# Experts of a two-layer decoder on one core: from split float32r products to plain float32 products on column tiles

## The chip, the cores and the metric

One core of a Trainium2 chip runs the whole program. The metric is the time of one execution on the device in microseconds (us); each number of a run is one execution, and a profile is one execution more, recorded instruction by instruction. Engines: TensorE (PE, with its weight loads as PEld), VectorE (DVE), ScalarE (ACT), GpSimd (POOL) and SyncE (SP), whose queue issues the loads.

## The reference

Two layers of a decoder over 256 tokens of 1024 channels. Each layer has four attention mixers and then a feed-forward part; in layer 0 that is a SwiGLU, in layer 1 it is eight SwiGLU experts of hidden width 2816, of which each token uses the two with the highest router logits. The change is in the experts alone:

```python
def moe_swiglu(h, router_w, w1, w3, w2):
    xt = h.reshape(-1, d)
    logits = (xt @ router_w).astype(jnp.float32)
    top_v, top_i = lax.top_k(logits, TOP_K)            # 2 of 8
    gate = jax.nn.softmax(top_v, axis=-1)
    ...
    a = lax.ragged_dot(xs, w1, sizes)
    g = lax.ragged_dot(xs, w3, sizes)
    y = lax.ragged_dot(jax.nn.silu(a) * g, w2, sizes)
    y = y * gate.reshape(-1)[order][:, None]
    return jnp.zeros_like(xt).at[tok].add(y)
```

Everything is float32. With the inputs of the reference the experts get 56, 55, 64, 69, 62, 65, 64 and 77 tokens.

## The kernel before, in words

Layer 1's experts are the function `moe`. It finds each token's two experts, gives every token a slot in each of them (`pos`), and **gathers** the tokens of two experts at a time by products with one-hot matrices (`onehot`, `gather`): `X(e)` is 1024 channels (8 blocks of 128) by 128 slots. An expert's 2816 hidden columns are worked in 11 steps of 256 (`j`); 88 pairs (expert, step) follow each other in the list `pairs`.

One step goes **up**, turns, and goes **down**. `up_half` multiplies the 128 slots (stationary operand) with the step's columns of `w1` and `w3` side by side (moving, 512 columns) over the 8 channel blocks into one PSUM bank `uv`. ScalarE and VectorE make silu(a) * g of it (`es`). `flip_act` turns the 128 x 256 result by two transposes (`at`), and `down` multiplies it with the step's 256 rows of `w2`, into two banks `y` that add up over the 11 steps. Behind the last step `scale_y` weights the rows with the gates, and `scatter_steps` adds them to the tokens (`scm`, then `xT`). The order is written out by hand: while step i goes up, step i-1 is turned between the halves of the up products and goes down after them; the flips, the scatter of the expert before and the gather of the next two hang on the lists `side` and `more`, one piece per step.

**Precision.** PE's fast type float32r keeps fewer bits than float32. So every operand is split into a high and a low float32r part, and every product is made of three (`mm3`, line 645: high by high, high by low, low by high). A weight tile comes from HBM as `raw` (128 x 2048 floats, 1 MiB); the class `Stream` loads the tiles in the order of a list `plan` into slots as these come free, and splits them in halves ahead of need (`ensure`): ScalarE writes `wh`, VectorE `wl = raw - wh`. The slot is free when its second half is split.

```python
    self.clk.sc.activation(wh[:, :hn], src, AF.Copy)
    self.clk.dv.tensor_tensor(wl[:, :hn], src, wh[:, :hn].bitcast(F32), op=OP.subtract)
```

**More than 128 tokens.** At the very end `mxv`, the largest count, is read into a register (line 1878), and a branch on all engines (line 1879) works slots 128 to 255 of every expert if it is above 128. With these inputs it is jumped over.

A recording layer (`Clock`, `Timed`) notes every operation, so nearly all instructions have line 385 in the profile; they are told apart by their tiles' names.

Of the kernel before, what the change touches and what calls it, by code (L numbers as in the profile page):

```python
# [26 lines left out]
P = 128  # L28
# [9 lines left out]
SLOTS = 128  # L38
NEG = -1e30
# [98 lines left out]
class Stream:  # L138
# [4 lines left out]
    def __init__(self, clk, plan):  # L143
# [7 lines left out]
        for ci, (key, ap) in enumerate(plan):  # L151
            assert key not in self.index, key
            self.index[key] = ci
            self.pieces += [(key, 0), (key, 1)]
# [16 lines left out]
    def add_halves(self, pool, names, last=None):  # L171

        for n in names:
            self.limit["wh" + n] = len(self.plan) if last is None else self.index[last]
            self.wring.appendleft((pool, n))
            self.look += 1
# [50 lines left out]
    def ensure(self, upto):  # L227

        while self.nsplit < min(upto, len(self.pieces)):
# [5 lines left out]
            while self.limit["wh" + self.wring[0][1]] < self.index[key]:  # L235
# [4 lines left out]
            wh = pool.tile([P, CH // 2], F32R, name=f"wh{self.nsplit}", tag="wh" + tag)  # L240
            wl = pool.tile([P, CH // 2], F32R, name=f"wl{self.nsplit}", tag="wl" + tag)
# [256 lines left out]
def trunk(ctx, tc, A):  # L498
# [41 lines left out]
    def add_item(it):  # L540
# [11 lines left out]
        elif k == "w2":  # L552
            add(it, ko(A["ffn_w2"][0, it[2] * 256:(it[2] + 1) * 256]))
        elif k == "e13":
            add(it, A["moe_w13"][0, l, it[2], it[3]])
        elif k == "e2":
            add(it, ko(A["moe_w2"][0, l, it[2] * 256:(it[2] + 1) * 256]))
# [29 lines left out]
    NSLOT, NWH, NWX, NX = 3, 4, (0, 0), (4, 5)  # L587
# [217 lines left out]
    hh = cpool.tile([P, KD, S], F32R, name="hh")  # L805
    hl = cpool.tile([P, KD, S], F32R, name="hl")
# [819 lines left out]
    def moe(fp, nf, gap, consts):  # L1626
# [8 lines left out]
        xe = mb.tile([P, 2, KD, SLOTS], F32R, name="xe", tag="merged")  # L1635
        half = lambda e: 0 if e % 2 == 0 else 1 + e // 2 % 2

        def X(e):

            if half(e) == 2:  # L1640
                return xe[:, 0], xe[:, 1]
            c = slice(half(e) * SLOTS, (half(e) + 1) * SLOTS)
            return hh[:, :, c], hl[:, :, c]
# [32 lines left out]
        st.move("aux")  # L1676
        for d in range(4, KD):
            flip(d)
# [24 lines left out]
        st.presplit(("e13", 0, 0, 1), 2)  # L1703
# [3 lines left out]
        cnti = fp.tile([P, 1], I32, name="cnti")  # L1707

        def gates():
# [3 lines left out]
            dv.tensor_copy(cnti, cnt[:, 0:1])  # L1713
            dv.tensor_tensor(w[:, :, 1:2], t8[:, :, 1:2], t8[:, :, 0:1], op=OP.subtract)
# [13 lines left out]
        def flip_oh(e, tag, res):  # L1728

            def f():  # L1730
                ps = pt(f"rt{tag}{e}")
                for i in range(2):
                    pe.matmul(ps[:, i * P:(i + 1) * P], ohv[:, i, e % 2], idr, start=True, stop=True)
                for i in range(2):
                    pe.matmul(ps[:, S:S + 1], ohv[:, i, e % 2].bitcast(F32), gat[:, i, e:e + 1], start=(i == 0),
                              stop=(i == 1))
                ohT = ohs[:, 512 + e % 2 * S:512 + (e % 2 + 1) * S]
# [5 lines left out]

        def gather(e):

            def pick(b, n):
                def f():
                    first = e == 0
                    ps = (px if first and n else pt)(f"g{e}{b}{n}")
                    for t in range(2):  # L1750
                        d = 2 * b + t
                        for i in range(2):
                            pe.matmul(ps[:, t * S:(t + 1) * S], (th, tl)[n][:, i, d * P:(d + 1) * P],
                                      ohv[:, i].rearrange("p e s -> p (e s)"), start=(i == 0), stop=(i == 1))
                    v = ps.rearrange("p (t e s) -> p t e s", t=2, e=2)
                    for k in range(2):
                        o = X(e + k)[n][:, 2 * b:2 * b + 2, :]
                        if first and n:
                            dv.tensor_copy(o, v[:, :, k])
                        else:  # L1760
                            sc.activation(o, v[:, :, k], AF.Copy)
                return f

            return [pick(b, n) for b in range(4) for n in range(2)]
# [12 lines left out]
        def scatter_steps(yy, ohT, tag, final=None):  # L1777
            def part(b):
                def f():
                    ps = pt(f"sc{tag}{b}")  # L1780
                    yh, yl = yy[b // 2]
                    for t in range(2):
                        o = ((2 * b + t) % 4) * P
                        pe.matmul(ps[:, t * S:(t + 1) * S], yh[:, o:o + P], ohT, start=True, stop=False)
                        pe.matmul(ps[:, t * S:(t + 1) * S], yl[:, o:o + P], ohT, start=False, stop=True)
# [15 lines left out]
        state = {0: {}, 1: {}}  # L1801
# [4 lines left out]
        side = deque([lambda: (gap.fill(4 - gap.j), st.move("gap")), flip_oh(0, "m", state[0]), lambda: deque(gap.end(), 0), flip_oh(1, "m", state[1])])  # L1806
        more = deque()
        ybanks, acts, atT = {}, {}, {}

        def up_half(e, j, c, ps):  # L1810

            Xh, Xl = X(e)
            for h, (wh, wl) in enumerate(st.halves(("e13", e, j, c))):
                whv = wh.rearrange("p (k n) -> p k n", k=2)
                wlv = wl.rearrange("p (k n) -> p k n", k=2)
                for k in range(2):
                    kk = 4 * c + 2 * h + k
                    mm3(ps, Xh[:, kk, :], Xl[:, kk, :], whv[:, k, :], wlv[:, k, :],
                        start=(kk == 0), stop=(kk == KD - 1))

        def flip_act(e, j):
            a = acts.pop((e, j))
            p2 = pt(f"at{e}_{j}")
            for t in range(2):
                pe.transpose(p2[:, t * P:(t + 1) * P], a[:, t * P:(t + 1) * P], ident)
            at = sm.tile([P, 512], F32R, name=f"ath{e}_{j}", tag="sq", bufs=3)
            ath, atl = at[:, 0:256], at[:, 256:512]
            sc.activation(ath, p2[:, 0:256], AF.Copy)
            dv.tensor_tensor(atl, p2[:, 0:256], ath.bitcast(F32), op=OP.subtract)
            atT[(e, j)] = (ath, atl)  # L1830

        def down(e, j):
            if j == 0:
                ybanks[e] = [px(f"y{e}_{n}") for n in range(2)]
            ath, atl = atT.pop((e, j))
            for h, (wh, wl) in enumerate(st.halves(("e2", e, j))):
                for n in range(2):
                    mm3(ybanks[e][n], ath[:, h * P:(h + 1) * P], atl[:, h * P:(h + 1) * P],
                        wh[:, n * 512:(n + 1) * 512], wl[:, n * 512:(n + 1) * 512],
                        start=(j == 0 and h == 0), stop=(j == NF - 1 and h == 1))  # L1840

        for i, (e, j) in enumerate(pairs):
            if j == 0 and e % 2 and e + 1 < NE:
                more.append(lambda e=e: onehot(e + 1, 0))
                more.extend(gather(e + 1))
            ps = pm(f"uv{e}_{j}")
            up_half(e, j, 0, ps)
            if i:
                flip_act(*pairs[i - 1])
            up_half(e, j, 1, ps)  # L1850
            s = sm.tile([P, 512], F32, name=f"es{e}_{j}", tag="sq", bufs=3)[:, 0:256]
            sc.activation(s, ps[:, 0:256], AF.Silu)
            dv.tensor_tensor(s, s, ps[:, 256:512], op=OP.mult)
            acts[(e, j)] = s
            if side:
                side.popleft()()
            if i:
                e2, j2 = pairs[i - 1]
                down(e2, j2)
                if j2 == NF - 1:  # L1860
                    yy = scale_y(ybanks.pop(e2), state[e2]["gs"], f"m{e2}")
# [219 lines left out]
```

## Time and profile before

| | us |
|---|---|
| runs of the kernel (median of 3) | 1577.34, 1573.70, 1574.76 (1574.76) |
| the profiled execution's own time | 1573.86 |
| its span, first to last instruction | 1572.1 |
| PE busy | 1532.2 (97%) |
| DVE busy | 1272.2 (81%) |
| ACT busy | 1037.2 (66%) |
| mean granted TensorE clock | 0.993 of full speed |

Busy time is the time in which an engine had at least one instruction under way; overlapping matmuls are not counted twice, while a mean of one counts each from its start to its end. So "mean 392" beside a product every 235 ns means that they overlap. "128*64" in a row of PE is rows by columns of the stationary operand, "128x256" what is written. Idle time of an engine that bounds nothing costs nothing.

### The profile page before, as it was taken

The numbers are of one execution on the slowest core, as the hardware profiler recorded it, in microseconds if no ns is written. First come the engines' busy times: TensorE is split into PE (matmuls) and PEld (weight loads), VectorE is DVE, ScalarE is ACT, GpSimd is POOL, SyncE is SP. The second block draws the span as 40 slices with busy tenths as digits, with TensorE's granted clock in tenths as the row PEclk, the third lists the DMA queues.
The fourth block names the chain that finished last, engine by engine and source line by source line (L and its number), as shares of the span: only waits on it lengthen the run. The fifth ranks groups of instructions, "written<-read, shape, count | busy, mean of one in ns | idle before, by whom it ended". The sixth has DMA issues, their size and how long they took to land.

```text
span 1572.1 us, 25486 instructions
## 1 busy us (share of the span) xinstructions
PE 1532.2 (97%) x10164; PEld 1352.0 (86%) x10164; DVE 1272.2 (81%) x1646; ACT 1037.2 (66%) x1452; POOL 56.2 (4%) x58
## 2 busy tenths in 40 slices
PE   7999998999999999999999999999999999999996
PEld 6998998899998999989778888888888888888885
DVE  4797787666656786776689989999899998999996
ACT  3546553544444546554678888888888888888884
POOL 0000013000001000012000000000000000000000
PEclk9999999999999999999999999999999999999998
DMA  9565656977633765539789999999899999999960
GB/s 370 222 232 185 223 207 245 367 269 252 233 135 113 258 215 188 188 135 355 288 334 371 356 338 365 357 363 354 330 365 356 365 355 335 359 363 363 366 243 29
DMA packets 84878, 445.99 MB, mean 284 GB/s; under 512 B 8080, under 2 KB 8464, under 8 KB 51344
## 3 DMA queue, kind: packets, MB, share of 16 engines
q1 hardware_dynamic: 84032, 443.71, 76.0%
q8 instruction: 81, 1.33, 0.3%
q10 hardware_dynamic: 720, 0.59, 0.1%
q14 instruction: 45, 0.37, 0.1%
HBM read 443.22 MB, written 1.05 MB: 283 GB/s over the span
## 4 chain that ended last, share of the span: by engine, by line
PE 79%; issue 15%; DVE 3%; DMA 1%; ACT 1%; POOL 1%; SPq 0%; DVEq 0%; POOLq 0%; ACTq 0%
PE uv L385 31%; PE y L385 15%; PE mg L385 11%; PE pt L385 7%; PE br L385 2%; PE at L385 1%; PE wo L385 1%; PE g L385 1%; PE scm L385 1%; DVE wl L385 1%; PE pcq L385 1%; PE ada L385 1%; PE pck L385 1%; PE oa L385 1%; DMA aux<-in_nsa_ck_w 0%
## 5 line engine op out<-in xcount | busy, mean ns | idle before, releaser
L385 DVE TENSOR_TENSOR wl<-raw,wh 128x1024 fp32r<-128x1024 f32 x738 | 883.9, 1228 | 168.7 <-ACT wh L385 157.0
L385 ACT ACTIVATE wh<-raw 128x1024 fp32r<-128x1024 f32 x738 | 769.7, 1056 | 142.6 <-PE uv L385 18.5
L385 PE MATMUL y<-wh,ath 128*128 128x512 f32 x704 | 232.9, 392 | 0.5 <-ACT ath L385 0.5
L385 PE MATMUL uv<-wh,hh 128*128 128x512 f32 x528 | 212.9, 403 | 0.0
L385 PE MATMUL uv<-wh,hl 128*128 128x512 f32 x528 | 207.0, 392 | 0.0
L385 PE MATMUL uv<-wl,hh 128*128 128x512 f32 x528 | 206.7, 392 | 0.0
L385 PEld LDWEIGHTS y<-wh,ath 128*128 128x128 f32 x704 | 132.1, 188 | 28.1 <-ACT ath L385 0.7
L385 PE MATMUL mg<-hh,wh 128*128 128x256 f32 x512 | 147.0, 287 | 0.8 <-DVE brt L385 0.8
L385 PE MATMUL mg<-hh,wl 128*128 128x256 f32 x512 | 143.5, 280 | 4.2 <-DVE wl L385 4.2
L385 PE MATMUL mg<-hl,wh 128*128 128x256 f32 x512 | 143.0, 279 | 0.0
L385 PE MATMUL y<-wl,ath 128*128 128x512 f32 x352 | 137.6, 391 | 0.0
L385 PE MATMUL uv<-wh,xe 128*128 128x512 f32 x352 | 119.1, 401 | 0.0
L385 PEld LDWEIGHTS uv<-wh,hl 128*128 128x128 f32 x528 | 99.1, 188 | 22.5
L385 PEld LDWEIGHTS uv<-wh,hh 128*128 128x128 f32 x528 | 99.2, 188 | 18.5
L385 PEld LDWEIGHTS uv<-wl,hh 128*128 128x128 f32 x528 | 99.4, 188 | 18.0
L385 PEld LDWEIGHTS mg<-hh,wl 128*128 128x128 f32 x512 | 96.5, 188 | 4.9 <-DVE wl L385 4.8
L385 PEld LDWEIGHTS mg<-hh,wh 128*128 128x128 f32 x512 | 96.6, 189 | 3.0 <-issue 2.0
L385 PEld LDWEIGHTS mg<-hl,wh 128*128 128x128 f32 x512 | 96.7, 189 | 1.0 <-issue 1.0
L385 PE MATMUL pt<-wh,hh 128*128 128x256 f32 (+1 forms) x320 | 90.3, 282 | 0.0
L385 PE MATMUL pt<-wl,hh 128*128 128x256 f32 (+1 forms) x320 | 89.2, 279 | 0.0
L385 PE MATMUL pt<-wh,hl 128*128 128x256 f32 (+1 forms) x320 | 89.2, 279 | 0.0
L385 PEld LDWEIGHTS uv<-wh,xe 128*128 128x128 f32 x352 | 66.2, 188 | 14.5
(417 smaller groups left out, 2837.5 us busy)
## 6 DMA issues: line engine op xcount, KB each, us to landing
raw<-in_moe_w SPq DMA_DIRECT2D x263, 1024.0 KB, 5.1
raw<-in_w_in SPq DMA_DIRECT2D x54, 1024.0 KB, 5.1
aux<-in_w_ada SPq DMA_DIRECT2D x48, 1024.0 KB, 7.4
raw<-in_ffn_w SPq DMA_DIRECT2D x33, 1024.0 KB, 5.4
raw<-in_w_branch SPq DMA_DIRECT2D x8, 1024.0 KB, 5.4
raw<-in_w_out SPq DMA_DIRECT2D x8, 1024.0 KB, 5.0
raw<-in_w_in_tail SPq DMA_DIRECT2D x2, 576.0 KB, 4.0
xT<-in_x SPq DMA_DIRECT2D x1, 1024.0 KB, 6.2
```

The costliest lines, as they stand in the source:

```text
L385: r = f(*args, **kw)
```

## The change

It does six things, all in layer 1's experts but for the tile of the split halves.

1. **Plain float32 products.** The expert weights (`e13`, `e2`) are no longer split; PE reads the raw tiles. `X(e)` is one float32 tile, gathered in one piece. A slot is freed (`raw_done`) when the products that read it are done.
2. **Two column tiles.** 64 slots (`BASE`) are the stationary operand of the base products. A step's 256 columns are two groups of 128 (`w1` and `w3` together 256 moving columns); group 0 stands on columns 0 to 63 of the array and writes partitions 0 to 63, group 1 on columns 64 to 127. Going down, the same with the two halves of the step's hidden columns.
3. **Arms.** Slots 64 to 95 and 96 to 127 are worked in two nested arms of 32 slots, on four column tiles, per block of two steps. Their products stand behind a comparison with the expert's own count (`regs[e]`, loaded into a register of PE alone); the other engines don't branch, they turn and evacuate the arms' banks (`uvo`, `yo`), which are cleared first, either way. An expert has 11 such places: 6 blocks, one last down part, four parts of the scatter.
4. **Slots.** The four tiles of split halves (now one tile `w` each) and `merged` become slots of the raw tiles in this stage; the tiles of the feed-forward pool are 4 instead of 5.
5. **Layout.** `moe_w13` and `moe_w2` are laid out anew on the host side so that a tile is 128 rows of 8 KB and the two groups are contiguous.
6. The early splits (`presplit`) of the first expert tiles are left out.

```diff
+BASE, MORE = 64, 32
+RAW = ("e13", "e2")
...
+            if key[0] not in RAW:
+                self.pieces += [(key, 0), (key, 1)]
...
-    NSLOT, NWH, NWX, NX = 3, 4, (0, 0), (4, 5)
+    NSLOT, NWH, NWX, NX = 3, 4, (0, 0), (4, 4)
...
+        st.add_slots(wpool, [f"w{i}" for i in range(NWH)])
+        st.add_slots(mb, ["merged"])
...
+        def flip_more(e, res):
...
+                for r in range(2):
+                    oh = columns(e, f"o{r}{e}", BASE + r * MORE, MORE)
+                    ps = pt(f"ro{r}{e}")
+                    for i in range(2):
+                        pe.matmul(ps[:, i * P:(i + 1) * P], oh[:, i], idr, start=True, stop=True)
...
+                    base(0)
+                    if rest is not None:
+                        reg, yo, oho = rest
+                        q = slice(MORE * b, MORE * (b + 1))
+
+                        def add(r):
+                            for t in range(2):
+                                pe.matmul(ps[:, t * S:(t + 1) * S], yo[q, r * S + t * P:r * S + (t + 1) * P],
+                                          oho[q, r, :], start=False, stop=False, tile_position=(MORE * b, 0))
+
+                        arms(reg, add)
+                    base(1)
...
+        def arms(reg, work, back=False):
+
+            with tc.If(reg > BASE):
+                if not back:
+                    work(0)
+                with tc.If(reg > BASE + MORE):
+                    work(1)
+                if back:
+                    work(0)
...
         def up_half(e, j, c, ps):
 
-            Xh, Xl = X(e)
-            for h, (wh, wl) in enumerate(st.halves(("e13", e, j, c))):
-                whv = wh.rearrange("p (k n) -> p k n", k=2)
-                wlv = wl.rearrange("p (k n) -> p k n", k=2)
-                for k in range(2):
-                    kk = 4 * c + 2 * h + k
-                    mm3(ps, Xh[:, kk, :], Xl[:, kk, :], whv[:, k, :], wlv[:, k, :],
-                        start=(kk == 0), stop=(kk == KD - 1))
+            x = X(e)
+            for kk in range(4 * c, 4 * c + 4):
+                w = raw13(e, j, kk)
+                for t in range(2):
+                    pe.matmul(ps[t * BASE:(t + 1) * BASE, 0:S], x[:, kk, 0:BASE], w[:, t], start=(kk == 0),
+                              stop=(kk == KD - 1), tile_position=(0, t * BASE))
...
-            for h, (wh, wl) in enumerate(st.halves(("e2", e, j))):
-                for n in range(2):
-                    mm3(ybanks[e][n], ath[:, h * P:(h + 1) * P], atl[:, h * P:(h + 1) * P],
-                        wh[:, n * 512:(n + 1) * 512], wl[:, n * 512:(n + 1) * 512],
-                        start=(j == 0 and h == 0), stop=(j == NF - 1 and h == 1))
+            at, w = atT.pop((e, j)), raw2(e, j)
+            for n in range(2):
+                for t in range(2):
+                    pe.matmul(ybanks[e][n][t * BASE:(t + 1) * BASE, :], at[:, t * BASE:(t + 1) * BASE],
+                              w[:, t, n * 512:(n + 1) * 512], start=(j == 0), stop=(j == NF - 1),
+                              tile_position=(0, t * BASE))
+
+        def up_more(e, b, ps):
...
+                lo = BASE + r * MORE
+                for kk in range(KD):
+                    for p, j in enumerate(blocks[b]):
+                        w = raw13(e, j, kk)
+                        for t in range(2):
+                            g = MORE * (2 * p + t)
+                            pe.matmul(ps[g:g + MORE, r * S:(r + 1) * S], x[:, kk, lo:lo + MORE], w[:, t],
+                                      start=(kk == 0), stop=(kk == KD - 1), tile_position=(0, g))
...
+        def down_more(e, b):
...
+                for p, j in enumerate(blocks[b]):
+                    w = raw2(e, j)
+                    for t in range(2):
+                        k = MORE * (2 * p + t)
+                        for q in range(4):
+                            pe.matmul(yo[MORE * q:MORE * (q + 1), r * S:(r + 1) * S], at[:, r, k:k + MORE],
+                                      w[:, t, q * S:(q + 1) * S], start=(b == 0 and k == 0 and r == 0),
+                                      stop=(b == len(blocks) - 1 and k == MORE and r == 0),
+                                      tile_position=(0, MORE * q))
...
         for i, (e, j) in enumerate(pairs):
+            if j == 0:
+                regs[e] = nc.values_load(cnte[0:1, e:e + 1], engines=(mybir.EngineType.PE,), min_val=0, max_val=S)
...
+            b, last = j // 2, j in (blocks[j // 2][-1],)
+            if last:
+                pso = pm(f"uvo{e}_{b}")
+                dv.memset(pso, 0.0)
...
+                arms(regs[e], work)
+                act_more(e, b, pso)
+                for jj in blocks[b]:
+                    for c in range(2):
+                        st.raw_done(("e13", e, jj, c))
             if i:
                 e2, j2 = pairs[i - 1]
                 down(e2, j2)
+                if last and b:
+                    done2(e, b - 1)
...
+                    arms(regs[e2], down_more(e2, len(blocks) - 1), True)
...
-            st.presplit(("e13", 0, 0, 0))
```

The order of the instructions changes on PE in every step. Before, in the second half of the up products of expert 0's step 1 and its way down (`rtm` is a flip of the one-hots), PE has one product after the other on the whole array:

```order
L385 MATMUL uv_1_9012<-wh_9013,hh 128x512
L385 MATMUL uv_1_9012<-wl_9014,hh 128x512
L385 MATMUL uv_1_9012<-wh_9013,hl 128x512
L385 MATMUL rtm_9066<-idr,ohs 128x128 x2
L385 MATMUL rtm_9066<-gat,ohs 128x1 x2
L385 MATMUL y_0_9074<-wh_9025,ath_0_9038 128x512
L385 MATMUL y_0_9074<-wl_9026,ath_0_9038 128x512
L385 MATMUL y_1_9075<-wh_9025,ath_0_9038 128x512
```

Now, from that place on to the end of step 2 (`at` and `ao` are the turns of the base and of the arms; the row of eight is four channel blocks by two column tiles):

```order
L393 MATMUL uv_1_8772<-raw_8203,x_8688 64x256 x8
L393 MATMUL rtm_8798<-idr,ocm_8796 128x128 x2
L393 MATMUL rtm_8798<-gat,ocm_8796 128x1 x2
L1850 COMPARE_AND_BRANCH
L1850 UNCONDITIONAL_BRANCH
L393 MATMUL y_0_8883<-raw_8211,at_0_8783 64x512 x2
L393 MATMUL y_1_8884<-raw_8211,at_0_8783 64x512 x2
L393 MATMUL uv_2_8889<-raw_8271,x_8688 64x256 x8
L393 MATMUL at_1_8898<-cst,es_1_8793 128x128
L393 MATMUL ao_0_8902<-cst,so_0_8872 128x128 x2
L393 MATMUL uv_2_8889<-raw_8331,x_8688 64x256 x8
```

The 36 products of a step have become 20, each of the 20 on half of the array's columns. Between the comparison and the branch that ends it stand the arms, 64 rows that are left out here; in a full block (expert 0, block 1) an arm begins and ends like this, with 32 products `uvo` and 16 `yo` per arm:

```order
L1850 COMPARE_AND_BRANCH
L393 MATMUL uvo_1_8929<-raw_8271,x_8688 32x256 x2
L393 MATMUL uvo_1_8929<-raw_8614,x_8688 32x256 x2
L393 MATMUL yo_8770<-raw_8211,ato_0_8905 32x256 x8
L393 MATMUL yo_8770<-raw_8612,ato_0_8905 32x256 x8
L1853 COMPARE_AND_BRANCH
```

A count of at most 64 jumps from the first comparison over both arms; a count of 65 to 96 runs through the first and jumps at the second. In the order, a float32 product stands once; in PE's instruction stream it is two weight loads and two matmuls, so both arms of a full block are 388 instructions with their branches.

## Rows read from the trace of the kernel before

**Rows 1.** The page: busy us by engine, then GB/s in 40 slices.
```profile
span 1572.1 us, 25486 instructions
...
PE 1532.2 (97%) x10164; PEld 1352.0 (86%) x10164; DVE 1272.2 (81%) x1646; ACT 1037.2 (66%) x1452; POOL 56.2 (4%) x58
...
GB/s 370 222 232 185 223 207 245 367 269 252 233 135 113 258 215 188 188 135 355 288 334 371 356 338 365 357 363 354 330 365 356 365 355 335 359 363 363 366 243 29
```

**Rows 2.** The expert stage as one stretch (its first line names the columns).
```profile
core 0: us, PE busy (x) PEld busy (x) DVE busy (x) ACT busy (x) POOL busy (x), PEclk, DMA share, GB/s
777.00:1558.00 781.00, 778.63 (x3606) 640.16 (x3605) 711.91 (x768) 647.08 (x831) 0.00 (x0) 1.00 0.90 335
```

**Rows 3.** Groups of PE by shape: count | busy us, mean ns.
```profile
L385 PE MATMUL at<-cst,es 128*128 128x128 f32 x176 | 33.5, 271 | 0.0
...
L385 PE MATMUL ws<-kT,ar 128*128 128x256 f32 x8 | 2.1, 380 | 0.0
...
L385 PE MATMUL ws1a<-kT,ar 128*128 128x512 f32 x4 | 2.0, 592 | 0.0
```

**Rows 4.** Timeline of PE, expert products: start, length, tile<-operands, count.
```profile
1541.50 0.63 PE L385 MATMUL uv<-wh,xe 128*128 128x512 f32 x2
1541.97 0.40 PE L385 MATMUL uv<-wl,xe 128*128 128x512 f32 x1
```

**Rows 5.** Timeline of PE: float32 products on four column tiles (adag).
```profile
752.83 0.28 PE L385 MATMUL wo<-mh,wl 128*128 128x256 f32 x1
753.04 1.07 PE L385 MATMUL adag<-aux,cact 128*32 128x256 f32 x16
754.04 0.27 PE L385 MATMUL npsf<-cst,sqf 128*128 128x1 f32 x1
```

**Rows 6.** Timeline of PE: float32 products on two column tiles (od).
```profile
203.14 1.58 PE L385 MATMUL od<-Td,vt 128*64 128x128 f32 x24
```

**Rows 7.** The line of the branch: ns shortest/median/longest, first and last start.
```profile
L1879 POOLq COMPARE_BRANCH  x1: 45/45/45, 778.5 to 778.5; - x1
...
L1879 PEldq COMPARE_BRANCH  x1: 3795/3795/3795, 1561.5 to 1561.5; - x1
```

**Rows 8.** The line that reads the count into a register.
```profile
L1878 SPq FUSED_REGOPS  x1: 194/194/194, 1518.1 to 1518.1; - x1
...
L1878 PEldq TENSOR_LOAD <-cnti x1: 488/488/488, 1560.9 to 1560.9; - x1
```

**Rows 9.** The page's part 3: instruction fetch, packets and MB.
```profile
q8 instruction: 81, 1.33, 0.3%
```

**Rows 10.** DMA queue's waits, 800 to 1500: us in total, times, longest.
```profile
SPq L385 <- DVE wl L385: 600.4, 237, 3.8
```

**Rows 11.** Stretches as in rows 2: loads queued deep, and expert stage.
```profile
725.00:730.00 5.00, 5.00 (x44) 4.96 (x43) 3.61 (x6) 3.06 (x4) 3.01 (x3) 1.00 1.01 423
730.00:735.00 5.00, 5.00 (x41) 4.67 (x40) 5.00 (x4) 2.30 (x4) 3.13 (x2) 1.00 1.01 392
900.00:910.00 10.00, 10.00 (x50) 8.28 (x50) 9.03 (x10) 8.57 (x13) 0.00 (x0) 1.00 0.92 333
```

**Rows 12.** A stretch as in rows 2, in which the clock fell.
```profile
760.00:765.00 5.00, 5.00 (x43) 2.59 (x44) 4.30 (x12) 4.01 (x9) 1.47 (x2) 0.56 1.00 419
```

**Rows 13.** Timeline of PE at the same place.
```profile
759.91 3.64 PE L385 MATMUL adag<-aux,cact 128*32 128x256 f32 x32
763.49 0.38 PE L385 MATMUL rl<-hh,rwh 128*8 128x256 f32 x1
```

**Rows 14.** Timeline of PE, last scatter.
```profile
1558.76 0.28 PE L385 MATMUL scm<-ohs,yhm 128*128 128x256 f32 x1
1558.88 0.28 PE L385 MATMUL scm<-ohs,ylm 128*128 128x256 f32 x1
...
1561.37 0.28 PE L385 MATMUL scm<-ohs,ylm 128*128 128x256 f32 x1
```

More of the change, by code (lines that the diff above doesn't have):

```diff
@@ L173, in add_halves @@
         for n in names:
-            self.limit["wh" + n] = len(self.plan) if last is None else self.index[last]
+            self.limit["w" + n] = len(self.plan) if last is None else self.index[last]
             self.wring.appendleft((pool, n))
@@ L1634, in moe @@
         dv.tensor_tensor(rwl, rw, rwh.bitcast(F32), op=OP.subtract)
-        xe = mb.tile([P, 2, KD, SLOTS], F32R, name="xe", tag="merged")
-        half = lambda e: 0 if e % 2 == 0 else 1 + e // 2 % 2
         def X(e):
[L1640 to L1643, printed above, removed]
+            if e not in xs:
+                n = "hh" if e // 2 % 2 == 0 else "hl"
+                xs[e] = xs[e + 1] = cpool.tile([P, KD, S], F32, name=f"x{e}", tag=n)
+            return xs[e][:, :, e % 2 * SLOTS:(e % 2 + 1) * SLOTS]
+        xs = {}
         th = fp.tile([P, 2, D], F32R, name="th")
@@ L1762, in pick @@
                 return f
-            return [pick(b, n) for b in range(4) for n in range(2)]
+            return [pick(b) for b in range(4)]
         def scale_y(banks, gs, tag):
@@ L1781, in f, with base @@
                     yh, yl = yy[b // 2]
[L1782 to L1785, printed above, removed]
+                    def base(n):
+                        for t in range(2):
+                            o = ((2 * b + t) % 4) * P
+                            pe.matmul(ps[:, t * S:(t + 1) * S], (yh, yl)[n][:, o:o + P], ohT, start=(n + t == 0),
+                                      stop=(n + t == 2))
+                    base(0)
[8 more added lines that the diff above has]
+                    base(1)
                     if final is None:
@@ new lines, in moe, with raw13, raw2 @@
+        blocks = [tuple(range(j, min(j + 2, NF))) for j in range(0, NF, 2)]
+        def raw13(e, j, kk):
+            return st.raw(("e13", e, j, kk // 4)).rearrange("p (k t n) -> p k t n", k=4, t=2)[:, kk % 4]
+        def raw2(e, j):
+            return st.raw(("e2", e, j)).rearrange("p (t n) -> p t n", t=2)
+        def up_half(e, j, c, ps):
+            x = X(e)
[4 more added lines that the diff above has]
+                              stop=(kk == KD - 1), tile_position=(0, t * BASE))
@@ L1821, in flip_act @@
         def flip_act(e, j):
-            a = acts.pop((e, j))
             p2 = pt(f"at{e}_{j}")
[L1824 to L1830, printed above, removed]
+            pe.transpose(p2[:, 0:P], acts.pop((e, j)), ident)
@@ new lines, in act_more, with flip_more_act @@
+        def act_more(e, b, ps):
+            v = ps.rearrange("p (r n) -> p r n", r=2)
+            s = sm.tile([P, 512], F32, name=f"so{e}_{b}", tag="sq", bufs=3)[:, 0:S].rearrange("p (r n) -> p r n", r=2)
+            sc.activation(s, v[:, :, 0:P], AF.Silu)
+            dv.tensor_tensor(s, s, v[:, :, P:S], op=OP.mult)
+            actso[(e, b)] = s
+        def flip_more_act(e, b):
+            a = actso.pop((e, b))
+            p2 = pt(f"ao{e}_{b}")
+            for r in range(2):
+                pe.transpose(p2[:, r * P:(r + 1) * P], a[:, r], ident)
+            at = atTo[(e, b)] = fp.tile([P, 2, P], F32, name=f"ato{e}_{b}", tag="ato", bufs=2)
+            sc.activation(at, p2[:, 0:S].rearrange("p (r n) -> p r n", r=2), AF.Copy)
@@ new lines, in done2, with finish @@
+        def done2(e, b):
+            for j in blocks[b]:
+                st.raw_done(("e2", e, j))
+        def finish(e):
+            yy = scale_y(ybanks.pop(e), state[e]["gs"], f"m{e}")
+            yo, src, gso = fp.tile([P, 512], F32, name=f"yo{e}", tag="yo"), yobank.pop(e), state[e]["gso"]
+            for r in range(2):
+                sc.activation(yo[:, r * S:(r + 1) * S], src[:, r * S:(r + 1) * S], AF.Copy, scale=gso[:, r:r + 1])
+            r = state.pop(e)
+            return scatter_steps(yy, r["ohT"], f"m{e}", e == NE - 1 or None, (regs[e], yo, r["oho"]))
@@ L1871, in moe @@
         flip_act(e, NF - 1)
+        flip_more_act(e, len(blocks) - 1)
         down(e, NF - 1)
-        yy = scale_y(ybanks.pop(e), state[e]["gs"], f"m{e}")
-        for f in scatter_steps(yy, state[e]["ohT"], f"m{e}", True):
+        arms(regs[e], down_more(e, len(blocks) - 1), True)
+        done2(e, len(blocks) - 1)
+        for f in finish(e):
             f()
```

126 lines of the change are left out of this document (79 added, 47 removed).

## The prediction

> **What bounds the kernel now.** I read the page first, then the windows, then the groups and the timeline of PE, and last the queue's waits. On the page PE is busy for 1532 of 1572 us, and in the second half the loads run near 360 GB/s [rows 1]. Both look like a limit, so the expert stage has to be read alone. From the first up product to the last down product it takes 781 us; PE is busy for 778.6 of them at the full clock, the loads keep the DMA engines 0.90 busy at 335 GB/s, and VectorE and ScalarE, which split the weights, are busy for 712 and 647 us [rows 2]. Which of PE and the loads waits for the other is told by the queue: between 800 and 1500 us it waited 600 us for VectorE to have split a tile and freed its slot [rows 10]. The loads are held back; with many queued they ran at 392 to 423 GB/s, against 333 in a stretch of the stage [rows 11]. So PE's order of products bounds the stage, with little air behind it: at 36 products per step of 256 hidden columns, one every 0.235 us [rows 4], 88 steps take 744 us.
>
> **What a product costs after.** The plain float32 product shows in the trace as two weight loads and two matmuls: the order has four `ws` products and the group shows eight records [rows 3]. A record of 512 columns lasts 592 ns, one of 256 lasts 380: 212 ns for 256 columns, so a whole float32 product of 256 columns streams for 425 ns, and one of 512 for 850. Alone that would be the end of it, since three products with split operands take 0.7 us for 512 columns by 128 slots. What decides is whether products on different column tiles run side by side. On four tiles sixteen records of 256 columns went through in 1.00 us (753.04 to 754.04), where one after the other they need 16 x 0.212 = 3.4 us [rows 5]; on two tiles 24 records of 128 columns took 1.58 us with the last one's tail, where singly they need 24 x 0.106 = 2.5 [rows 6]. I take full overlap, four or two at the price of one.
>
> **The change, part by part.**
> - Base, slots 0 to 63: 16 products of 256 columns going up are 32 records, two abreast: 16 x 0.212 = 3.4 us; 4 products of 512 going down are 8 records, two abreast: 4 x 0.425 = 1.7 us. 88 steps x 5.1 = 451 us.
> - Arms. The reference's router, worked out with its inputs, gives the experts 56, 55, 64, 69, 62, 65, 64 and 77 tokens. So three experts (3, 5 and 7) take the first arm, and none takes the second, which begins at 97. An arm's up part is 64 records of 256 columns, four abreast, in each of 6 blocks (the last with 32 records, two abreast): 6 x 3.4 = 20 us; its down part 16 records per step: 11 x 0.85 = 9.4; its scatter 8 products on one row tile after the other: 3.4. Three times 33 is 100 us.
> - Turns, gather, scatter and the flips of the one-hots: 184 turns (88 and two per block) and 368 short records at 0.12 us [rows 14]: 66 us. The turns stay at about two per step, the flips grow threefold; gather and scatter stay.
> - Changes of tile. Going from whole-array products to column tiles cost 0.21 us to the next start instead of 0.12, and 1.00 us for 4 x 0.212 on the way out [rows 5]; about 0.1 each. Along the path that these counts take, the order has 348 changes in the stage: 35 us.
> - Branches. 11 arms per expert, 88 in all. An arm that is not taken ends in a wait of PE for its own last product, so PE runs dry: the part of a record that its successor otherwise covers (592 - 425 = 167 ns, rows 3), two branches at the 45 ns that the hit on POOL took [rows 7], and a restart like a change of tile, together 0.4 us. 88 x 0.4 = 35 us. An arm that is taken has the same at its inner branch. The register that holds the count is loaded once per expert, 0.49 and 0.19 us [rows 8]: 5.5 us.
> - ScalarE's and VectorE's splits of the expert weights go: 528 of each, from a path that PE covered, so nothing is counted. If PE gets faster they would have been the bound; now they aren't.
>
> 451 + 100 + 66 + 35 + 35 + 6 = 693 us, against 781.
>
> **Code that isn't there.** This is the unknown cost, and the trace has its two ends: PE's one branch at the end of the program, over some 13,700 instructions, held it for 3.8 us, and POOL's, over one, for 0.045 [rows 7]. PE executes 20,300 weight loads and matmuls here [rows 1] and fetches 81 times [rows 9], a block of some 250 instructions at a time. Each untaken arm of a full block skips 388 instructions (96 products of four, and the branches), two others per expert 260, the rest 69 or 20. If PE holds its block and the next one, the least with which straight code can run, a skip of 388 lands outside with a chance of (388 - 256)/256, half; one of 260 almost never. The five experts that take no arm have 20 such skips: ten misses. The ends are none and all 30 skips of 260 and more. I take ten, because the far row is a miss and the skip is longer than a block; at 4 us each, 40 us.
>
> The Trainium skill, "Runtime: NRT & Kernel Launch", section "Instruction fetch mechanics", says that a branch out of a two-page window stalls for the fetch of its page, with strictly sequential prefetch; no stretch of this trace shows how much is held. By that rule the sum has the ten misses, and it is the argument against putting such arms there at all.
>
> **Loads.** An expert is 33 MiB, 34.6 MB: 83 us at 415 GB/s. The stage now has 17 slots of 1 MiB for the raw tiles (3, 4, 1, 4, the four that held split halves, and `merged`), held until the products are done instead of until the split. An expert without arms costs PE about 74 us and is overtaken by the loads' pace after the head start of 17 tiles (42 us) is spent, near the third expert; one with arms costs 107 and gives the time back. I count 6 us. At 392 GB/s it is 88 us, and still the arms cover it.
>
> **Before and after the stage.** Up to the routing the order on every engine is the same but for two neighbours on the load queue; the early splits of the first expert tiles are left out there, off PE's path. I count nothing; bounds are some us either way. Behind the last down product come the scatter with its four arms and the output; from the last scatter to the end it is 10.7 us (1561.4 to 1572.1, rows 14 and 1), and the four parts now wait for each other through branches: 4 us.
>
> **The sum.** 777 + 693 + 6 + 4 + 10.7 = 1491 us of span without misses, 1531 with ten. The profiled run took 1573.9 us at a span of 1572.1 and lies 0.9 under the median, so add 2: **1533 us**, 2.7% faster than the median of 1574.8. What this kernel's measurement can tell from no change is about 0.2%, 3 us.
>
> **The rivals.**
> - *No misses.* PE holds enough code that a skip of 388 is inside. For it: PE fetches 16 KB at a time and runs far ahead; nothing shows two blocks to be all. Time: 1533 - 40 = 1493.
> - *Every long skip misses: slower.* The place is the branch of each block of the five experts without arms. 30 misses at 4 us make 120 us, 80 more than I count: 1613. It decides from about 20 misses on. PE's clock adds to it: at 760 us it was granted at 0.56, between its levels of 1.2 and 2.4 GHz, after a stretch of one-column products and waits [rows 12], and 32 records took 3.6 us instead of 2.0 [rows 13]; with 1.6 us more per miss the point falls to 15. Against it: a skip of 260 ends in the next block, which straight code needs anyway.
> - *Neighbours on the array slow each other: slower.* If all of the 1.58 us of rows 6 is stream time, a step of two records costs 0.132 instead of 0.106, and 551 us of tiled products become 24% longer: +132, 1665. Rows 5 speak against it, with four abreast at nearly full pace. The Trainium skill, "TensorE: Matmul & The Clock Gate", section "Part 3: Packing small matmuls", measures only 2.38 times for three column tiles; rows 5 show 3.4 for four, so I keep the rows.
> - *The loads stay near 360 GB/s* even with a deep queue. 96 us per expert, 769 - 42 = 727 us against PE's 733 with misses: both stall in turn, some 1550.
>
> **Numbers.** Forecast 0.45, own range 1505 to 1565 (stalls on banks that I left out, the clock after a miss, five misses more or fewer). No misses 0.27. All long skips miss 0.08, neighbours 0.05. Loads 0.07. The rest, 0.08, is spread, most of it on the fast side. Range 1478 to 1575, which leaves out the two slower rivals and little below. Faster by over 0.2%: 0.84; within 0.2%: 0.03; slower: 0.13.
>
> **What would show it.** In the new profile: `uv` records start two per 0.21 us, `y` two per 0.43; the stage lasts 690 to 740 us; the branch line shows 88 entries on PE, most under 0.2 us and some ten between 3 and 5; experts 3, 5 and 7 are 30 to 35 us longer than the others; the loads reach 400 GB/s in the first three. I am wrong in the mechanism if the base products take more than 0.25 us per pair, if over 20 or no branches stall, or if PE's idle time is ended by loads rather than branches.

## The result and the profile after

The change made the kernel slower: 1649.7 us in the median of four runs (1641.5 to 1652.6) against 1575.1 us before, a ratio of 1.046 with a 95% interval of 1.042 to 1.050. The forecast was 1533 us and faster. The profiled execution took 1650.3 us at a span of 1648.5.

The page, and after it the groups of the expert stage (columns as in the rows above):

```profile
span 1648.5 us, 28665 instructions
PE 1496.1 (91%) x12252; PEld 1115.4 (68%) x12252; DVE 678.9 (41%) x1183; ACT 520.9 (32%) x1012; POOL 56.3 (3%) x58
PEclk9999999999999999998899898899998999988998
q8 instruction: 156, 2.56, 0.6%
```

```profile
L393 PE MATMUL uv<-raw,x 128*64 128x256 f32 x2816 | 356.8, 395 | 10.1 <-issue 5.2 <-DVE gw L393 1.8 <-PEq L1850 1.2
L393 PE MATMUL y<-raw,at 128*64 128x512 f32 x704 | 193.6, 673 | 71.9 <-PEq L1850 54.0 <-ACT so L393 8.8 <-issue 6.3
L393 PE MATMUL uvo<-raw,x 128*32 128x256 f32 x1056 | 71.1, 405 | 0.0
```

Against [rows 1] VectorE and ScalarE lost half their work, as they should. But PE, 97% busy before, is at 91%, and its clock has 8s in the second half, where it had 9s. Fetches of instructions went from 81 [rows 9] to 156 packets. The largest idle time stands ahead of `y`, the down products, and it is ended by the branch of line 1850.

The stage by expert (columns: busy time and records of each engine, PE's granted clock, share of the DMA engines, GB/s):

```profile
783.00:870.00 87.00, 70.64 (x468) 38.37 (x470) 11.57 (x37) 11.15 (x36) 0.00 (x0) 0.90 0.78 311
870.00:972.00 102.00, 84.52 (x529) 45.84 (x525) 16.57 (x40) 17.38 (x51) 0.00 (x0) 0.90 0.84 340
972.00:1068.00 96.00, 77.87 (x499) 41.51 (x497) 15.01 (x37) 16.68 (x50) 0.00 (x0) 0.91 0.90 369
1068.00:1186.00 118.00, 110.36 (x1041) 60.17 (x1041) 17.14 (x41) 18.52 (x54) 0.00 (x0) 0.96 0.76 305
1186.00:1292.00 106.00, 85.38 (x529) 44.09 (x529) 14.47 (x35) 16.52 (x49) 0.00 (x0) 0.89 0.79 318
```

Experts 0, 1, 2 and 4 take no arm and last 87 to 106 us, with PE idle for 16 to 21 of them and the clock at 0.89 to 0.91. Expert 3 takes the first arm and has twice the records, but only 8 us idle and a clock of 0.96. So the experts that skip are the ones that lose time. The whole stage lasts 845 us (783 to 1628) where 733 with misses, plus 6 for the loads, was forecast; before, it was 781 [rows 2]:

```profile
783.00:1628.00 845.00, 730.03 (x5676) 393.53 (x5676) 123.62 (x306) 134.70 (x396) 0.00 (x0) 0.93 0.77 310
```

So PE is busy for 730 us of it and idle for 115.

One such skip, close to (windows ahead of it, in it, behind it, and after that):

```profile
951.00:960.00 9.00, 9.00 (x70) 4.74 (x66) 0.77 (x2) 1.16 (x4) 0.00 (x0) 1.00 1.01 425
960.00:964.50 4.50, 0.03 (x2) 0.03 (x1) 0.29 (x1) 0.45 (x2) 0.00 (x0) 1.00 0.57 235
964.50:968.00 3.50, 3.50 (x10) 1.29 (x12) 0.91 (x2) 0.21 (x1) 0.00 (x0) 0.52 0.76 255
968.00:978.00 10.00, 9.69 (x78) 5.76 (x76) 0.70 (x2) 1.66 (x6) 0.00 (x0) 1.00 1.02 428
```

PE is full at clock 1.00, stands still for 4.5 us, and then runs at 0.52, that is almost wholly at 1.2 GHz, before the 2.4 return. In the timeline of PE the same place reads:

```profile
959.64 0.39 PE L393 MATMUL uv<-raw,x 128*64 128x256 f32 x2
964.50 3.61 PE L393 MATMUL y<-raw,at 128*64 128x512 f32 x8 [4.47 <-PEq L1850]
967.83 2.03 PE L393 MATMUL uv<-raw,x 128*64 128x256 f32 x16
```

Eight `y` records take 3.61 us there, and 1.94 where the clock is full. A fetch of instructions began at 961.65 and took 1.02 us; the trace of DMA packets has such a fetch 2.3 to 2.9 us before the end of each of the 22 stands that are counted below. The packet itself takes 1.0 us; what fills the rest of that time no run tells.

The waits of the stage (total us, times, longest):

```profile
PE y L393 <- PEq L1850: 54.0, 26, 4.7
PE ro L393 <- DVE oco L393: 17.7, 16, 1.1
PE rtm L393 <- DVE ocm L393: 8.9, 8, 1.1
PE y L393 <- ACT so L393: 8.8, 15, 0.8
PE y L393 <- issue: 6.3, 2, 4.4
PE uv L393 <- issue: 5.2, 4, 1.8
```

And SP's queue:

```profile
SPq L393 <- PEq L1850: 411.9, 35, 26.3
SPq L393 <- PEq L1853: 224.2, 15, 23.2
SPq L393 <- DMA raw<-in_moe_w: 6.4, 6, 2.3
```

The loads wait for PE, not PE for them. That leaves three suspects (theory A): stands around skips, the waits of the flips `rtm` and `ro` for one-hots, and the lower clock behind both. Going through the stage skip by skip, 18 of the 20 skips of 388 places have a stand of PE of 0.6 to 4.8 us at the branch or within the next step, and 4 of the 10 skips of 260: 22 stands, 63 us together. Fifteen of them are at the branch, seven in straight code shortly behind it: the six that end by "issue" above, and one of 0.75 us that the profile puts down to a load, though a fetch began 2.6 us before its end as well. The clock: 845 us at a mean of 0.93 is 118 us at half speed, which would cost 59 if PE had been busy throughout; it was idle for a part of that time, so this is an upper bound (the expectations below take in the end of the program as well, with 136 and 68). The rivals: products side by side are dearer than forecast (B), or each branch empties the array at a high price, however far it goes (C).

### The profile page after: what moved, and what is told of

The parts are those of the page before. It is cut to its first block, busy times and chain, and to the rows that moved or that the text cites. A ratio compares the mean times of both kernels' runs of the same rounds, so it can differ in the third digit from the quotient of the medians.

```text
span 1648.5 us, 28665 instructions
## 1 busy us (share of the span) xinstructions
PE 1496.1 (91%) x12252; PEld 1115.4 (68%) x12252; DVE 678.9 (41%) x1183; ACT 520.9 (32%) x1012; POOL 56.3 (3%) x58
## 5 line engine op out<-in xcount | busy, mean ns | idle before, releaser
L393 PE MATMUL uv<-raw,x 128*64 128x256 f32 x2816 | 356.8, 395 | 10.1 <-issue 5.2
L393 PEld LDWEIGHTS uv<-raw,x 128*64 128x64 f32 x2816 | 210.8, 142 | 153.4 <-issue 75.4
L393 DVE TENSOR_TENSOR w<-raw,w 128x1024 fp32r<-128x1024 f32 (+1 forms) x210 | 258.1, 1242 | 106.1 <-ACT w L393 105.5
L393 PE MATMUL y<-raw,at 128*64 128x512 f32 x704 | 193.6, 673 | 71.9 <-PEq L1850 54.0
L393 ACT ACTIVATE w<-raw 128x1024 fp32r<-128x1024 f32 (+1 forms) x210 | 217.3, 1047 | 105.8 <-PE fa L393 16.6
L393 PE MATMUL mg<-hh,w 128*128 128x256 f32 x1024 | 189.0, 284 | 4.9 <-DVE w L393 4.2
L393 PEld LDWEIGHTS mg<-hh,w 128*128 128x128 f32 x1024 | 158.6, 189 | 7.9 <-DVE w L393 5.0
L393 PE MATMUL mg<-hl,w 128*128 128x256 f32 x512 | 143.0, 279 | 0.0
L393 PE MATMUL pt<-w,hh 128*128 128x256 f32 (+1 forms) x640 | 113.8, 280 | 0.0
L393 PEld LDWEIGHTS pt<-w,hh 128*128 128x128 f32 x640 | 97.7, 188 | 1.4 <-issue 1.4
L393 PE MATMUL uvo<-raw,x 128*32 128x256 f32 x1056 | 71.1, 405 | 0.0
```

The costliest lines, as they stand in the source:

```text
L393: r = f(*args, **kw)
```

## The experiments

**e1, one-hots ahead.** `columns` is called five steps earlier for `rtm`, one step earlier for `ro`, each in a tile of its own:

```diff
-                oh = columns(e, f"{tag}{e}", lo, n)
+                oh = res.pop("oc") if "oc" in res else columns(e, f"{tag}{e}", lo, n)
...
-                    oh = columns(e, f"o{r}{e}", BASE + r * MORE, MORE)
+                    oh = res["oco"][:, r]
...
-                    side.append(lambda: None)
+                    side.append(lambda e=e: state[e].update(oc=columns(e, f"m{e}", 0, BASE)))
```

> The one-hots that the flips of the routing need are built one step of the queue earlier (and in tiles of their own), so that TensorE finds them ready; arms and products stay. Theory A (the stage is 855 us where 733 was forecast because TensorE stands still and its clock then drops: 63 us of idle time at 22 places around the long skips, 27 us in 24 waits of the flips of about 1.1 us each, and 136 us spent at half the clock after such idle times, which costs 68 us): the 27 us go, and the stretches at half clock that follow a flip alone go too (54 us of them begin at a flip, so up to 27 us): 1600 to 1625 us. Theory B (the products side by side cost more than forecast; the idle times only stand where work would wait anyway): under 10 us, 1640 to 1650. Theory C (each branch empties the array, and that is what costs): the same as B for this run, 1640 to 1650 less the 27 us at the most.

Measured: 1603.3 us, 1.017 times the kernel before (1.014 to 1.020), 46 us less than the change. The two waits of the flips are gone from the list, 26.6 us; the stage shrank by 47, to 798 us. So another 20 us came from the clock: the same number of records kept PE busy for 709 us instead of 730, at a mean clock of 0.96 instead of 0.93. The stage, and `y <- PEq`, which is as it was:

```profile
781.00:1579.00 798.00, 709.34 (x5676) 383.42 (x5676) 122.86 (x307) 134.88 (x396) 0.00 (x0) 0.96 0.81 329
PE y L393 <- PEq L1855: 52.4, 23, 6.0
```

**e2, one arm only.** It leaves the second arm away and keeps every outer branch:

```diff
             with tc.If(reg > BASE):
-                if not back:
-                    work(0)
-                with tc.If(reg > BASE + MORE):
-                    work(1)
-                if back:
-                    work(0)
+                work(0)
```

> The second arm (slots 96 to 127, which no expert of these inputs fills) is left out, with its inner branch; so the long skips of an expert that takes no arm are half as long (194 places in TensorE's stream instead of 388) and the number of outer branches is the same. Theory A (the skips land in code that has to be fetched): of the 63 us of idle time around the skips at least two thirds go, with the clock's drops behind them (about 80 us at half clock, so 40 us), and 10 us of inner taken branches: 1545 to 1590 us. Theory C (a branch empties the array, however far it goes): only the inner branches go, 1630 to 1645. Theory B (products cost more than forecast): 1630 to 1650.

Measured: 1537.6 us, 0.976 times before (0.973 to 0.979): 112 us by taking away products that never ran and the inner branch in front of them. Its stage and the waits in it:

```profile
779.00:1512.00 733.00, 690.93 (x5676) 377.34 (x5676) 123.22 (x306) 133.12 (x396) 0.00 (x0) 0.98 0.88 358
PE ro L393 <- DVE oco L393: 17.7, 16, 1.1
PE rtm L393 <- DVE ocm L393: 8.9, 8, 1.1
PE y L393 <- PEq L1850: 7.8, 25, 0.4
```

25 waits at the branch, about as many as before, but of 0.31 us each instead of 2.1: what the branch over an arm costs when its target is there. PE is busy for 39 us less with as many records, at a clock of 0.98 instead of 0.93. Theory C is out.

The fetches tell one thing more. The change needs 156 packets; e2, and e3 below, need fewer:

```profile
q8 instruction: 121, 1.98, 0.5%
```

The second arm is some 1100 instructions per expert (half of four skips of 388, two of 260 and the short ones), 8900 in all, and the 35 packets that are gone held some 250 each, 8750. So PE had fetched nearly all of the second arm, though it never ran it: here a skip spares the products, but not the fetch.

**e3, both edits.**

The diffs are those of e1 and e2.

> Both edits together: one arm only (slots 96 to 127, which these inputs do not fill, are left out) and the one-hots of the flips built ahead. Theory A: the gains add, and hardly any idle time over 1 us is left in the stage, so hardly any half clock: 1500 to 1550 us, faster than the kernel before. Theories B and C: 1600 to 1640.

Measured: 1501.8 us, 0.953 times before (0.950 to 0.956). The stage, and its two large groups:

```profile
783.00:1481.00 698.00, 677.81 (x5674) 370.43 (x5670) 121.20 (x304) 132.59 (x395) 0.00 (x0) 1.00 0.92 375
```

```profile
L393 PE MATMUL uv<-raw,x 128*64 128x256 f32 x2816 | 340.1, 383 | 7.5 <-DMA raw<-in_moe_w 3.7 <-DVE gw L393 1.8 <-PEq L1855 1.2
L393 PE MATMUL y<-raw,at 128*64 128x512 f32 x704 | 169.7, 601 | 10.4 <-PEq L1855 7.3 <-ACT so L393 1.2 <-DMA raw<-in_moe_w 0.9
L393 PE MATMUL uvo<-raw,x 128*32 128x256 f32 x1056 | 65.8, 380 | 0.0
```

It executes the same products. They were busy for 46 us more in the change (356.8 + 193.6 + 71.1 against 340.1 + 169.7 + 65.8): that is the clock, seen on the records themselves. Over all records of the stage it is 730 against 678, 52 us. And 698 us is what the forecast's sum gives without misses, 693 and 6. Theory B is out.

**e4, no arms.** The body of `arms` goes, so slots 64 to 127, which three experts use, are left out:

```diff
-            with tc.If(reg > BASE):
...
+            return
```

> No arms at all: slots 64 to 127 are left out, which three of the eight experts use; no branch in the stage. Theory A: against the change 100 us of arm products, 63 us of idle time around skips, some 40 us of half clock behind them and 15 us of short branches go: 1420 to 1450 us; the flips' 24 waits and the clock's drops behind them stay. Theory B (the base products themselves cost more than the 451 us and the 66 us of turns that were forecast): 1480 us or more. Theory C: as A.

Measured: 1434.3 us in one run, inside what theories A and C give. No branch is left in the stage, and the waits of the flips stay at 17.7 and 8.9 us. Something new shows, in the list of waits:

```profile
PE uv L393 <- DMA raw<-in_moe_w: 14.4, 33, 1.0
```

The loads run at 410 GB/s over the stage and are the bound in places, for some 14 us. A packet of instructions takes 1.07 us in the median there and in the stage of the change alike, so the loads do not slow the packet itself.

**e5, the arm for all experts.** In `arms`, on top of e1:

```diff
-            with tc.If(reg > BASE):
...
+            work(0)
```

> As e3_one_arm_ahead, with the one arm executed for all eight experts and no branch in the stage (slots 96 to 127 are left out). Five arms more at 33 us each, and some 50 branches less at 0.2 to 0.4 us: theory A gives 1640 to 1665 us, slower than the kernel before, so the branch pays as long as it is short. If a branch costs far more than it shows (theory C), under 1600.

Measured: 1654.2 us, 1.050 (1.048 to 1.052). Its stage is 852 us with PE busy for 850, at clock 1.00:

```profile
782.00:1634.00 852.00, 849.97 (x8395) 460.58 (x8392) 122.64 (x304) 136.35 (x396) 0.00 (x0) 1.00 0.78 307
```

Against e3 that is 154 us for five arms: 31 us each net of their branches, against 33 counted. Skipping pays, as long as the skip is short.

**e6, a longer skip.** Dose and response: the second arm's products stand there twice and are never executed.

```diff
                 with tc.If(reg > BASE + MORE):
                     work(1)
+                    work(1)
```

> As e1_ahead, with the second arm's products written twice (never executed with these inputs): the untaken skip grows from 388 to some 580 places, and the inner skip of the three experts that take the first arm from 193 to some 385. Theory A: the outer skips now miss nearly all of 30 times, and the inner ones more than half of 18 times, at 3 to 4.5 us idle and about 2 us of half clock each: 1660 to 1780 us. Theories B and C: as e1_ahead, 1595 to 1610 us, since no instruction more is executed.

Measured: 1711.3 us, 1.086 (1.084 to 1.088), 108 us slower than e1 without one executed instruction more. The stage's mean clock falls to 0.91. Its waits and fetches are

```profile
PE y L393 <- PEq L1855: 98.9, 29, 4.9
PE y L393 <- PEq L1858: 7.8, 3, 2.8
q8 instruction: 186, 3.05, 0.7%
```

The fetches rise with the code that stands there, to 186 packets.

**e9, two skips one behind the other.** Two short skips instead of a long one:

```diff
-                with tc.If(reg > BASE + MORE):
-                    work(1)
...
+            def more():
+                with tc.If(reg > BASE + MORE):
+                    work(1)
```

> As e1_ahead, but the second arm stands behind the first under a branch of its own, not inside it: an expert that takes no arm makes two skips of 194 places, one right behind the other, where it made one of 388. Same work, same places in all. If what counts is how far the stream of instructions has to jump within a short time (the code behind it has not been fetched yet): no gain against e1_ahead, 1590 to 1615 us. If what counts is the length of a single skip: the gain of e2_one_arm, 1515 to 1545 us.

Measured: 1607.8 us, 1.021 (1.017 to 1.024), the time of e1, though in e2 the skips of 194 alone passed. So it is not the length of one skip that decides, but how far the stream has to jump before more code can come. In the timeline the first skip of a pair passes and the second stands:

```profile
1002.78 0.48 PE L393 MATMUL scm<-ohs,ylm 128*128 128x256 f32 x2 [0.56 <-PEq L1856]
1008.74 2.83 PE L393 MATMUL y<-raw,at 128*64 128x512 f32 x6 [5.48 <-PEq L1856]
```

**e10, work between the two skips.** `down` is put between the arms:

```diff
                 down(e2, j2)
+                if last:
+                    with tc.If(regs[e] > BASE + MORE):
+                        work(1)
+                    act_more(e, b, pso)
```

> As e9_two_skips, with the down products of the step (about 2 us) put between the two arms of a block, so that each skip of 194 places is followed by work. If the code behind a skip is fetched while the work between runs: most of the idle time goes, 1520 to 1560 us. If 2 us are too short for the fetch (in the trace of the change each wait ends some 2.6 us after a fetch began): in between, 1560 to 1600 us. If branches themselves cost: 1600 or more.

Measured: 1588.1 us, 1.008 (1.006 to 1.011): the case in between, which the expectation put at 1560 to 1600. The same place now:

```profile
998.41 1.94 PE L393 MATMUL y<-raw,at 128*64 128x512 f32 x8 [0.36 <-DMA raw<-in_moe_w]
1004.08 3.68 PE L393 MATMUL uv<-raw,x 128*64 128x256 f32 x16 [3.73 <-PEq L2008]
```

1.94 us of work hide some of the fetch, and 3.7 us of the 5 to 6 remain. How much work would hide it all was not tried. The edit also brought a wait that e9 doesn't have, for the arms' results, which are now evacuated later; so its time may say too little of what the work hides:

```profile
PE uv L393 <- DVE so L393: 29.2, 15, 4.6
```

**e8, a version for use.** One arm; `act_more`, `flip_more` and `flip_more_act` for one arm as well; the branch at the end takes slots from 96 on, in two passes:

```diff
-        with tc.If(mxv > SLOTS):
-            for e in range(NE):
+        with tc.If(mxv > BASE + MORE):
+            for off in (BASE + MORE, SLOTS):
+                for e in range(NE):
...
+                    if off == SLOTS:
+                        dv.memset(ohT[0:BASE + MORE, :].bitcast(F32), 0.0)
```

> A version for use: one arm, one-hots ahead, slots from 96 on handed to the branch at the end (two passes: slots 96 to 223, then 224 to 255), and the second arm's turns, flips and gates gone too (per expert six transposes, two flips of 128 columns and two columns of gates, about 1.3 us of TensorE). Against e3_one_arm_ahead (1501.8 us) some 8 x 1.3 = 10 us less where TensorE is the bound, less where the loads are: 1488 to 1502 us, faster than the kernel before by 4.5 to 5.5 per cent. If the last branch, which now skips twice the code, costs more: up to 1506.

Measured: 1494.3 us (1492.7 to 1496.1), 0.948 times before (0.946 to 0.950): 5% faster than before and 9% faster than the change. The last passes are not executed with these inputs. Its page, its stage and its queue of loads:

```profile
PE 1432.6 (96%) x12156; PEld 1081.1 (72%) x12156; DVE 666.3 (45%) x1167; ACT 501.3 (34%) x996; POOL 56.1 (4%) x58
GB/s 369 219 259 158 243 185 258 309 314 276 232 251 60 174 217 223 170 198 142 353 337 298 419 419 419 420 418 421 420 416 383 417 420 329 398 356 419 420 205 31
781.00:1472.00 691.00, 668.00 (x5578) 360.25 (x5574) 110.48 (x287) 115.26 (x380) 0.00 (x0) 1.00 0.92 379
```

```profile
SPq L393 <- DMA raw<-in_moe_w: 232.8, 115, 3.1
```

PE is nearly as busy as before the change [rows 1], for fewer us. The loads run at 420 GB/s in much of the stage and their queue waits for loads to land, but PE waits for them for only 7 us and is busy for 668 of the stage's 691: PE bounds it, with the loads close behind.

## Why the prediction was wrong

The sum against the profile: first product at 783 us instead of 777, stage 845 instead of 739, end 20.5 us behind the stage instead of 14.7. 6 + 106 + 6 is the whole miss of 118 us of span. Of the 106, 23 are the skips (63 us instead of 40), 27 the waits of the flips and 52 the clock, and some 4 are not assigned; the waits and the clock the forecast had at nothing. The steps that failed are therefore the count of misses, the flips without a wait, and a sum without the clock.

**Right: the price of the work.** "I take full overlap, four or two at the price of one": e3's stage is 698 us where 451 + 100 + 66 + 35 + 35 + 6 and 6 for the loads gave 699. The total is nearer than its terms, which is in part luck: PE is busy for 678 us there, where products, turns and changes of tile make 652, and idle for 20, where branches, registers and loads make 47. In the change, wherever it ran at full clock, 16 `uv` records took 1.95 us with the tail (1.7 without by the forecast), and the 64 `uvo` of an arm 3.66 (3.4). The arms' 33 us measured 31 net of branches (e5). The branch that hits, 0.4 us, showed 0.31. The rival of neighbours on the array, at 1665 us, is out.

**Right: the loads.** SP waited 636 us for PE's branches in the change. In e3 PE waits 4.6 us for loads, where 6 were counted; in e4, at 410 GB/s, it waits 16.

**Wrong: the count under "Code that isn't there".** "[A] skip of 388 lands outside with a chance of (388 - 256)/256, half; one of 260 almost never", so "ten misses". There were 22 stands: 18 of 20 behind skips of 388, 4 of 10 behind those of 260. They cost 2.9 us each instead of 4, 63 instead of 40. e2, e6 and e9 show what it hangs on: with 194 places no stand over 0.6 us is left, with some 580 the wait at the branch nearly doubles, and two skips of 194 in a row are as bad as one of 388. So PE did not reliably hold the next block whole, as the model assumed (this is concluded from the counts; what PE holds no run shows directly), and even where the branch itself passed, the code behind it could be late: seven of the stands are in straight code. The Trainium skill, "Runtime: NRT & Kernel Launch", section "Instruction fetch mechanics", says that a branch whose target is outside the two pages held stalls for a fetch. The runs agree: a fetch began 2.3 to 2.9 us before the end of each of the 22 stands. The count of ten, drawn from two held blocks, was too low. "[I]f over 20 or no branches stall" was the forecast's own sign of a wrong mechanism, and 22 places did, 15 of them at the branch itself.

**Wrong: the clock was left out of the sum.** It stood in a rival as "1.6 us more per miss". It cost 52 us of the stage, the time for which PE was busy longer than in e3 with the same products. Taking away the flips' waits alone gave back 21 of PE's busy time (e1), taking away the long skips alone 39 (e2); the two overlap. Rows 12 had shown a clock of 0.56 after waits and one-column products; it belonged to the stands of 4 us that the forecast itself counted.

**Wrong: flips without their wait.** That "the flips grow threefold" was priced by their records alone. Each `columns` is built on VectorE when the flip asks for it, in one buffer, so PE waits 1.1 us three times per expert: 26.6 us, and 20 more by the clock that went with them (e1).

**The rival that came nearest** is "every long skip misses: slower", at 1613 us with the point of decision at 15 to 20 misses. It got a chance of 0.08, because the model of two whole blocks was taken for a fact, though no row showed it.

**The balance.** From the change to e3 the stage loses 147 us. PE's idle time falls by 95 (115 to 20): 47 at the branches of long skips, 11 in straight code, 27 in the flips and 11 at inner branches that are gone make 96, and the loads take back 2 or 3. Its busy time falls by 52 (730 to 678): the clock.

**Still open:** the 6 us ahead of the stage. Code and order on PE are the same there in all variants, and they reached the first product between 778.5 and 784.2 us, so a part of it is the spread from one execution to the next. Why the branch at a stand lasts 3.1 to 4.3 us in ten places and 6.0 to 6.4 in five no run tells. Of the 6 at the end the trace says only that PE ran at half clock from 1634 us on, with the scatter's branches and transfers between.

## What to carry to other kernels

Code that is jumped over is not free, even if it never runs: on this kernel a second arm that was never needed cost 112 us, some 11 of them at its inner branches, and leaving it out, which cut the skips from 388 to 194 instructions, gave them back. The fetches fit this: the second arm was fetched all the same. By e9 and e10 such a branch is to be judged by how far the stream jumps within a few microseconds, and the code for rare cases is better put at the end of the program, behind one branch, as in e8. Count with the stands of TensorE what the lower clock takes afterwards: here it took about as much as the stands at the branches did, and it makes small waits (1.1 us for a one-hot) worth removing.

## What was not expected of the hardware

- A fetch that comes late shows in two ways: 15 times as a branch of 3.1 to 6.4 us, and seven times as a stand in straight code, within a step behind a branch that seemed to pass in 0.3 to 1.1 us.
- At two waits of 1.1 us in the flips of an expert, 0.8 us apart, the granted clock fell to 1.2 GHz in all eight experts, during the second wait or up to 1.5 us behind it, as it did at stands of 4.5 us. At a single stand of 2.0 us (1201 us) it stayed at 2.4. Expert 2:

```profile
1036.00:1039.70 3.70, 1.81 (x16) 1.15 (x12) 0.93 (x4) 0.66 (x2) 0.00 (x0) 1.00 0.25 102
1039.70:1046.50 6.80, 4.21 (x14) 2.44 (x16) 0.76 (x3) 0.77 (x2) 0.00 (x0) 0.50 0.27 78
1046.50:1056.00 9.50, 9.50 (x75) 5.25 (x74) 0.77 (x2) 1.16 (x4) 0.00 (x0) 1.00 1.01 423
```

  In this stretch a stand of 2.3 us at a skip follows, and the clock is at 1.2 GHz from the second flip until the products have run for a while.
- Experts that take the arm wait 0.56 us at each inner branch and kept the full clock there (1.00 from 1080 to 1145 us); it fell in them at the flips.
